# Layer one's first projections on raw transposed tokens, with rstd applied at their evictions

## The chip, the cores and the metric

The kernel runs on one core of a Trainium2 chip. The metric is the device time of one execution in microseconds (us), the median of several runs. Lower is better.

## What is computed

Two residual layers on 256 tokens of width 1024. Each layer normalizes the stream (RMS norm), makes one wide projection of it, and cuts this into three token mixers and their gates; the mixers' outputs are projected, gated, merged and projected again. What matters here is the beginning of a layer and the last norm:

```python
def rms_norm(x, w):
    y = x * lax.rsqrt(jnp.mean(x * x, axis=-1, keepdims=True) + NORM_EPS)
    return y * w

for layer in range(DEPTH):
    h = rms_norm(x, norm_w[layer])
    proj = jnp.einsum('bsd,de->bse', h, w_in[layer])
    (a_xbc, a_z, a_dt, b_q, b_k, b_v, b_z, c_q, c_k, c_v, c_f, c_z, gates) = jnp.split(proj, split_at, axis=-1)
    y_a = mamba2_branch(a_xbc, a_z, a_dt, ...)
    y_b = sliding_window_branch(b_q, b_k, b_v, b_z, ...)     # rope on q and k
    y_c = forgetting_attention_branch(c_q, c_k, c_v, c_f, c_z, ...)
    ...
    x = x + jnp.einsum('bsd,de->bse', merged, w_out[layer])
return rms_norm(x, final_norm_w)
```

The factor of a token, rstd = 1/sqrt(mean(x*x) + eps), is one number per token. A projection of h is therefore the projection of x * w, times rstd.

## The kernel before

**Products.** Every fp32 operand of a large product is cut into a high half (a rounded copy, `hi`, made by ScalarE) and a low half (the rest, `lo`, made by VectorE, in the start by POOL for a part), and a product is three passes: high by high, low by high, high by low. `split` (L254 to L263) does the cutting. The tokens stand transposed, channels on the partitions, in `hTh` and `hTl`, one block of 128 tokens after the other (t = 0, 1), eight blocks of 128 channels each (k). `tok` makes a product with tokens on the output's partitions (24 matmuls, 256 or 512 columns), `chan` one with channels there (24 matmuls of 256 columns).

**Weights.** The weights are a stream of parts of 128 x 1024 numbers (0.5 MB). SP's queue loads them (`load_to`, L328) into a ring of six tiles, `feed` (L358) splits them, at most AHEAD = 4 parts ahead of their use, and `release` (L376) gives a part back and feeds the next when its last product has read it. A piece of 256 columns is two parts, one of 512 columns four.

**Order.** TensorE's order is that of the program (`manual_schedule`). `ops` lists the products by hand. Small jobs (transposes of q and k, softmax groups, group norms) are generators put in by `launch` with a delay; `pump` enters those that are due at the end of a product, and in the middle of one with 512 columns, by a clock that the program keeps for TensorE. `drain` forces a branch's jobs to their end. For the start (up to and with the first value product) VectorE, ScalarE and POOL go by the program's order as well; behind it they are scheduled by the compiler.

**The start (L1134 to L1182).** SP's queue loads x's first 128 tokens, the norm weights as a row broadcast to all partitions, x's second 128 tokens, then weights. 30 transposes of the identity keep TensorE busy. The first tokens' squares give rstd (`row_rstd`, a power on POOL and four small VectorE steps), VectorE scales the tokens by it and by the norm row (L1160), TensorE transposes them, `split` writes `hTh` and `hTl`. The same follows for the second tokens, whose scaling POOL and ScalarE share (L1162 to L1176); their transposes stand inside the first key product (`second_rows`). `dense` with `after` groups that product's passes by four channel blocks and calls `second_rows` after each 12 matmuls. The first two weight parts are split in halves of two blocks, by ScalarE (L1148) and by VectorE and POOL (L1149).

**Layer one's order before:** sliding-window keys (256 columns, t = 0, 1), values, queries (two pieces of 512 columns, each t = 0, 1), the small projection for dt and the forget gate (`u_small`), the sliding window's gate z (four pieces, `u_z`), then eight conv pieces of 256 columns (`u_conv`), with the forgetting attention's values `u_cv` (two pieces of 512) behind the second and the fourth, the first gate behind the fifth, and `split_late` with the first branch projection behind the seventh. The evictions of keys and queries apply the rotary table (`rope`, L460 to L468, three VectorE products out of PSUM); those of values are ScalarE copies. A sliding-window group (`swa_quad`) may enter once the first z product is there.

**The end.** `out_end` (L988 to L1015) adds the residual, squares the new row pieces (ScalarE), and after the third piece computes rstd; in the last layer it multiplies 512 columns on VectorE and 512 on ScalarE and writes both.

Of the kernel before, what the change touches and what calls it, by code (L numbers as in the profile page):

```python
# [11 lines left out]
F32 = mybir.dt.float32  # L12
# [4 lines left out]
P = 128  # L17
# [14 lines left out]
WARM = 30  # L32
# [11 lines left out]
def hybrid_trunk(  # L44
# [110 lines left out]

    tab = T("tab", [P, 1])
# [3 lines left out]
    nwb0 = T("nwb", [P, D])  # L160
# [112 lines left out]
    def dense(pt, ah, al, bh, bl, w, after=None, mid=None):  # L273


        passes = ((ah, bh), (al, bh), (ah, bl))
# [50 lines left out]
    def load_to(j):  # L327

        while state["load"] < min(j, len(stream)):
# [3 lines left out]
            raw = T("raw" if n > 32 else "L1", [P, kper, n])  # L333
            for c, ap in src:
                m = ap.shape[-1]
                nc.sync.dma_start(raw[:, :, c:c + m],
                                  ap.rearrange("(k p) c -> p k c", p=P)[:, k:k + kper, :])
# [61 lines left out]
    y0.nwb = nwb0  # L399
# [42 lines left out]
    def tok(ah, al, w, t, turn=True, mid=None, **kw):  # L442
# [3 lines left out]
        p = pmm()  # L446
# [13 lines left out]
    def rope(p, t):  # L460

        p4 = p.rearrange("p (h d) -> p h d", h=4)
        cos = bc(rope_sb[:, t, 0, :], 1, 4)
        a = T("L1", [P, 4, 64])
        tt(a, p4, cos, op=ALU.mult)
        b = T("L1", [P, 4, 64])
        tt(b[:, :, 0:32], p4[:, :, 32:64], bc(rope_sb[:, t, 1, 0:32], 1, 4), op=ALU.mult)
        tt(b[:, :, 32:64], p4[:, :, 0:32], bc(rope_sb[:, t, 1, 32:64], 1, 4), op=ALU.mult)  # L468
        return a, b

    def u_bkv(y, c0, t, after=None):

        def f(w):
            p = tok(y.hTh, y.hTl, w, t, turn=w.n == 512 or c0 > 0, after=after)
# [4 lines left out]
            if c0 > 0:  # L479
                act(halves(y.bv[:, t, :]), p, AF.Copy)  # L480
            elif w.n == 512:
                act(y.bv[:, t, :], p[:, 1, :], AF.Copy)
            if c0 == 0:
                a, b = rope(p if w.n == 256 else p[:, 0, :], t)
# [3 lines left out]
                launch(1, rest(kd), D_K)  # L488
# [10 lines left out]
    def u_bq(y, c0, t):  # L499

        def f(w):
            p = tok(y.hTh, y.hTl, w, t, turn=w.n == 512)
            for i in range(w.n // 256):
                if t == 0:
                    y.qT[c0 + i] = T("qt", [P, 2, S])
                a, b = rope(p if w.n == 256 else p[:, i, :], t)
                q = T("L1", [P, 4, 64])
                gtt(q, a, b, op=ALU.add)
                launch(1, rest(c0 + i, q.rearrange("p h d -> p (h d)")), D_Q)
# [90 lines left out]
    def swa_quad(y, c, qT):  # L600
        yield lambda: (1, 0) in y.zdone
# [220 lines left out]
    def u_cv(y, c, t):  # L822
        def f(w):
# [3 lines left out]
            act(halves(y.cv[:, t, c:c + w.n]), p, AF.Copy)  # L827
# [160 lines left out]
    def out_end(y, c, t, i, n, xo, p):  # L988
        sl = slice(c, c + n)
        with tc.high_priority():  # L990
            tt(halves(y.xn[:, t, sl]), p, halves(xo), op=ALU.add)
            sum_sq(y.xn, t, c, y.ss[t][:, i:i + 1], n)
# [224 lines left out]
```

## Time and profile before

| | us |
|---|---|
| median of 3 runs (lowest to highest) | 848.27 (846.58 to 848.31) |
| the profiled execution | 847.65 |
| its span in the trace | 845.9 |
| granted TensorE clock in it | 0.996 |
| busy: PE, DVE, ACT, POOL | 833.4, 642.3, 511.6, 104.5 |

The span runs from the first recorded instruction to the end of the last transfer; the execution's own time is somewhat longer. Engines in the profile: PE is TensorE's matmuls, PEld its weight loads, DVE VectorE, ACT ScalarE, POOL GpSimd, SP the queue that loads weights. A busy PE is not a PE at its peak, since the ends of pipelined matmuls are modelled. A line of the timeline has start, length, engine, source line, operation, what it writes and reads (with a count), and in brackets the engine's idle time before it and what ended that.

### The profile page before, as it was taken

What the parts mean: (1) busy time and instruction counts of PE and PEld (TensorE: products, weight loads), DVE (VectorE), ACT (ScalarE), POOL (GpSimd) and SP (SyncE); (2) the same over time, 40 slices, a digit from 0 to 9 for tenths busy, and PEclk for the clock granted to TensorE, in tenths of its full rate; (3) what the DMA queues carried; (4) which work ended last, traced back from release to release, by engine and by line L of the source; (5) the groups of instructions that cost most, each with busy time, mean ns of one, the idle gap of its engine ahead of it and who ended that gap; (6) DMA issues with size and microseconds to landing.
All of it is one profiled execution on the core that took longest, in us unless ns stands there. A gap on an engine that the chain in (4) does not pass through costs nothing.

```text
span 845.9 us, 15985 instructions
## 1 busy us (share of the span) xinstructions
PE 833.4 (99%) x5964; PEld 763.3 (90%) x5964; DVE 642.3 (76%) x1403; ACT 511.6 (60%) x1004; POOL 104.5 (12%) x134
## 2 busy tenths in 40 slices
PE   7999999999999999999999999999999999999996
PEld 7999898989999998888989998899899999988896
DVE  5777997998776679656788879879968667785665
ACT  6466777665666667435555667776557667654442
POOL 6310100000131010210014001000003110121000
PEclk9999999999999999999999999999999999999999
DMA  8666565666465545648676465465755555576632
GB/s 303 183 205 208 166 200 162 201 210 197 128 202 175 172 159 187 218 155 282 206 237 218 143 206 159 142 199 183 241 171 176 174 175 152 161 235 212 212 100 76
DMA packets 126638, 158.43 MB, mean 187 GB/s; under 512 B 12784, under 2 KB 88224, under 8 KB 126560
## 3 DMA queue, kind: packets, MB, share of 16 engines
q1 hardware_dynamic: 109456, 140.79, 52.9%
q10 hardware_dynamic: 17056, 16.49, 6.4%
q8 instruction: 47, 0.77, 0.4%
q14 instruction: 31, 0.25, 0.1%
q0 software_dynamic: 48, 0.13, 0.0%
HBM read 155.22 MB, written 2.16 MB: 186 GB/s over the span
## 4 chain that ended last, share of the span: by engine, by line
PE 95%; DMA 2%; ACT 0%; DVE 0%; issue 0%; POOL 0%; SPq 0%; POOLq 0%; DVEq 0%; ACTq 0%
PE mm L96 82%; PE mx L96 9%; PE mx L100 4%; DMA raw<-in_w_proj_dram 2%; DMA raw<-in_w_in_dram 1%; POOL lo L1149 0%; ACT hi L1148 0%; ACT hi L259 0%; ACT L L1008 0%; DVE L L260 0%; DVE L L935 0%; DVE L L934 0%; ACT L L259 0%; POOLq L1213 0%; ACT L L215 0%
## 5 line engine op out<-in xcount | busy, mean ns | idle before, releaser
L260 DVE TENSOR_TENSOR lo<-raw,hi 128x1024 fp32r<-128x1024 f32 x252 | 308.2, 1234 | 94.9 <-ACT hi L259 81.9
L96 PE MATMUL mm<-hi,L 128*128 128x512 f32 (+1 forms) x1344 | 373.9, 364 | 1.9 <-ACT hi L1148 1.4
L259 ACT ACTIVATE hi<-raw 128x1024 fp32r<-128x1024 f32 x252 | 263.2, 1056 | 93.0 <-PE mm L96 66.9
L96 PE MATMUL mm<-L,hi 128*128 128x256 f32 x1792 | 317.7, 278 | 0.0
L96 PEld LDWEIGHTS mm<-L,hi 128*128 128x128 f32 x1792 | 277.7, 192 | 6.8 <-issue 3.3
L96 PEld LDWEIGHTS mm<-hi,L 128*128 128x128 f32 x1344 | 241.5, 190 | 32.4 <-issue 2.7
L96 PE MATMUL mm<-L,lo 128*128 128x256 f32 x896 | 246.4, 275 | 0.0
L96 PE MATMUL mm<-lo,L 128*128 128x512 f32 (+1 forms) x672 | 241.3, 360 | 0.6 <-POOL lo L1149 0.6
L96 PEld LDWEIGHTS mm<-L,lo 128*128 128x128 f32 x896 | 171.9, 192 | 0.2
L96 PEld LDWEIGHTS mm<-lo,L 128*128 128x128 f32 x672 | 127.3, 190 | 15.4 <-POOL lo L1149 0.8
L862 POOL TENSOR_SCALAR_AFFINE_SELECT bias<-bias 128x128 f32<-128x128 f32 x64 | 35.7, 593 | 407.8 <-DMA bias<-cumd 232.7
L556 ACT ACTIVATE pp<-pp,nm 128x128 f32<-128x128 f32 (+1 forms) x128 | 56.5, 443 | 13.0 <-DVE nm L550 13.0
L693 DVE SCALAR_TENSOR_TENSOR L<-L,vec,L 128x255 f32<-128x255 f32 (+2 forms) x96 | 46.3, 482 | 4.8 <-ACT L L690 3.4
L96 PE MATMUL mx<-L,L 128*64 128x128 f32 (+1 forms) x384 | 34.4, 314 | 0.0
L886 ACT ACTIVATE L<-L 128x512 f32<-128x512 f32 x24 | 15.2, 632 | 30.2 <-DVE L L885 30.0
L568 DVE TENSOR_SCALAR pp<-pp,rsum 128x128 f32<-128x128 f32 (+1 forms) x128 | 32.1, 314 | 0.5
L696 ACT ACTIVATE L<-L 128x256 f32<-128x256 f32 x32 | 13.3, 417 | 31.4 <-DVE L L693 25.9
L96 PEld LDWEIGHTS mx<-L,L 128*64 128x64 f32 x384 | 22.9, 136 | 9.4 <-ACT pp L556 1.3
L777 ACT ACTIVATE L<-mm 128x256 f32<-128x256 f32 x48 | 18.1, 378 | 21.0 <-PE mm L96 21.0
L585 ACT ACTIVATE L<-mx 128x512 f32<-128x512 f32 x48 | 27.0, 596 | 2.7 <-PE mx L100 2.5
L100 PE MATMUL mx<-ident,pp 128*128 128x128 f32 x192 | 26.3, 273 | 0.0
L100 PE MATMUL mx<-ident,L 128*128 128x128 f32 x152 | 23.1, 279 | 1.6 <-DVE L L935 0.8
(173 smaller groups left out, 716.0 us busy)
## 6 DMA issues: line engine op xcount, KB each, us to landing
raw<-in_w_in_dram SPq DMA_DIRECT2D x200, 512.0 KB, 4.3
raw<-in_w_proj_dram SPq DMA_DIRECT2D x48, 512.0 KB, 5.6
raw<-in_w_out_dram SPq DMA_DIRECT2D x16, 512.0 KB, 5.1
L<-cumd ACTq DMA_DIRECT2D x8, 512.0 KB, 5.2
bias<-cumd ACTq DMA_DIRECT2D x16, 256.0 KB, 3.8
L<-in_gate_bias_dram ACTq DMA_DIRECT2D x12, 256.0 KB, 3.9
L<-in_x_dram SPq DMA_DIRECT2D x2, 512.0 KB, 5.0
nwb<-in_norm_w_dram SPq DMA_DIRECT2D x1, 512.0 KB, 5.4
```

Of the source, the lines that this page charges most:

```text
L96: nc.tensor.matmul(o, a, b, **kw)
L100: nc.tensor.transpose(o, a, i)
L259: keep(act)(hi, src, AF.Copy)
L260: keep(tt)(lo, src, hi.bitcast(F32), op=ALU.subtract)
L556: act(pp[:, i, sl], pp[:, i, sl], AF.Exp, scale=-1.0, bias=nm[:, e:e + 1], accum_out=sums[:, e:e + 1])
L568: ts(pp[:, i, sl], pp[:, i, sl], rs[:, 2 * i + b:2 * i + b + 1], 0.5, op0=ALU.mult, op1=ALU.mult)
L585: act(pT, pt, AF.Copy)
L693: stt(a[:, s:S], x_[:, 0:S - s], y.vec[:, 16 * j + u:16 * j + u + 1], a[:, s:S], op0=ALU.mult, op1=ALU.add)
L696: act(th, a, AF.Tanh)
L777: act(halves(th), p, AF.Tanh, scale=0.5)
L862: nc.gpsimd.affine_select(out=bias[:, i, dst], in_=bias[:, i, src], compare_op=ALU.is_ge, fill=NEG, base=0, pattern=[[-1, P]], channel_mul ...
L886: act(g, g, AF.Tanh, scale=0.5)
```

## The change

**In the start.** The broadcast norm row is gone. The norm weights come as eight rows of 128 on ScalarE's queue, one small transpose puts them on the partitions (`nwT`). x's first tokens load in two halves, then the first two weight parts (the first in two halves), then x's second tokens, then weights. The raw x is transposed; VectorE multiplies the transposed block by `nwT` as it leaves PSUM (`turn`, into `xw`), ScalarE and VectorE cut `xw` into high and low half. The squares come behind, and rstd for all tokens (`y0.rn`) after the first key product. 10 warm-up transposes instead of 30, and 10 more between the two halves of the first tokens.

**At the evictions.** While `y.rn` is set, `rope` multiplies by rstd and the table in one three-operand step, and the value copies take rstd as their scale. This holds for keys, values, queries and the first piece of the forgetting attention's values, which moves up behind the queries.

**Later.** `normalize` (a job launched behind the queries) spreads rstd over the partitions with two fp32 products, multiplies `xw` by it in place and writes a second pair `hTh`, `hTl`; `normalized` drains it before the small projection and switches over.

**Layer one's order.** The conv pieces have the second value piece behind the third, the first gate behind the fifth, `split_late` behind the seventh and the second entry of the gate list behind the eighth. Sliding-window groups no longer wait for the first z product in layer one, but for the switch. Layer two keeps its order.

**In the end.** The last layer's last square is VectorE's, the variance goes ahead of the scaling by the norm row, and the two shares become 640 and 384 columns.

The diff, cut to its core:

```diff
-WARM = 30
+WARM = 10
+FILL = 10
...
+    nw8 = T("L1", [NK, P])
+    nc.scalar.dma_start(nw8, norm_w[0:1, :].rearrange("o (k p) -> (o k) p", p=P))
...
-    nc.sync.dma_start(x0[:, 0, :], x2[0:P, :])
-    nc.sync.dma_start(nwb0, norm_w[0:1, :].to_broadcast([P, D]))
-    nc.sync.dma_start(x0[:, 1, :], x2[P:S, :])
+    for j in range(2):
+        nc.sync.dma_start(x0[:, 0, j * 512:(j + 1) * 512], x2[0:P, j * 512:(j + 1) * 512])
...
             if after is not None:
-                if i % 12 == 11:
-                    after[i // 12]()
+                after.get(i + 1, lambda: None)()
...
+            if y.rn is None:
+                tt(o, i, bc(r, 1, 4), op=ALU.mult)
+            else:
+                stt(o, i, y.rn[:, t:t + 1], bc(r, 1, 4), op0=ALU.mult, op1=ALU.mult)
...
-                act(halves(y.bv[:, t, :]), p, AF.Copy)
+                act(halves(y.bv[:, t, :]), p, AF.Copy, scale=y.rn[:, t:t + 1])
...
-                launch(1, rest(kd), D_K)
+                launch(1, rest(kd), D_K if y.rn is None else 2 * D_K)
...
     def swa_quad(y, c, qT):
-        yield lambda: (1, 0) in y.zdone
+        yield lambda: (1, 0) in y.zdone or (y.l == 0 and y.rn is None)
...
-            sum_sq(y.xn, t, c, y.ss[t][:, i:i + 1], n)
             last = y.l + 1 == L
+            if last and i == 2:
+                junk = T("L2", [P, 512])
+                nc.vector.tensor_tensor_reduce(out=junk[:, 0:n], in0=y.xn[:, t, sl], in1=y.xn[:, t, sl],
+                                               scale=1.0, scalar=0.0, op0=ALU.mult, op1=ALU.add,
+                                               accum_out=y.ss[t][:, i:i + 1])
+            else:
+                sum_sq(y.xn, t, c, y.ss[t][:, i:i + 1], n)
...
-                    ts(y.xn[:, t, 0:512], y.xn[:, t, 0:512], r[:, 0:1], None, op0=ALU.mult)
+                    m = 640
+                    ts(y.xn[:, t, 0:m], y.xn[:, t, 0:m], r[:, 0:1], None, op0=ALU.mult)
...
-            op(k, u_bkv(y, 0, 0, [lambda j=j: second_rows(j) for j in range(2)]))
-            op(k, u_bkv(y, 0, 1))
+            op(k, u_bkv(y, 0, 0, {16: lambda: second_rows(0), 20: lambda: second_rows(1)}, lambda: first_end()))
+            op(k, u_bkv(y, 0, 1, {}))
...
+            op(None, lambda: launch(9, normalize(y0), 0.0))
+            op(cols(C_CV, 512), u_cv(y, 0, 0), u_cv(y, 0, 1))
+            op(None, lambda: normalized(y0))
...
+        if l == 0:
+            lights = {2: [lambda: cv(512)], 4: [gp.pop(0)], 6: [lambda: op(None, lambda y=y: split_late(y, 1))],
+                      7: [gp.pop(0)]}
+        else:
+            lights = {1: [lambda: cv(0)], 3: [lambda: cv(512)], 4: [gp.pop(0)], 6: [gp.pop(0)]}
...
+    def normalize(y):
+        rb = T("L1", [P, S])
+        for t in range(2):
+            act(rb[:, t * P:(t + 1) * P], ident, AF.Copy, scale=y.rn[:, t:t + 1])
+        yield 2.0
+        p = pmx()
+        for t in range(2):
+            mm(p[:, t * P:(t + 1) * P], ones, rb[:, t * P:(t + 1) * P], start=True, stop=True)
+        hTh = T("L8", [P, 2, NK, P], F32R)
+        hTl = T("L8", [P, 2, NK, P], F32R)
+        for t in range(2):
+            for k in (0, 4):
+                xk = xw[:, t, k:k + 4, :]
+                tt(xk, xk, bc(p[:, t * P:(t + 1) * P], 1, 4), op=ALU.mult)
+                split(hTh[:, t, k:k + 4, :], hTl[:, t, k:k + 4, :], xk)
+        y.normal = hTh, hTl
+        yield 0.0
+
+    def normalized(y):
+        drain(9)
+        (y.hTh, y.hTl), y.rn = y.normal, None
...
+        load_to(2)
+        nc.sync.dma_start(x0[:, 1, :], x2[P:S, :])
         load_to(N_RAW)
...
+        def turn(t, j):
+            p = pmx()
+            for k in range(4):
+                c = j * 512 + k * P
+                transpose(p[:, k * P:(k + 1) * P], x0[:, t, c:c + P], ident)
+            ks = slice(4 * j, 4 * j + 4)
+            tt(xw[:, t, ks, :], p.rearrange("p (k t) -> p k t", k=4), bc(nwT[:, ks], 2, P), op=ALU.mult)
...
+        square(0, 0)
+        turn(0, 0)
+        w_high(parts[0], 0)
+        high(0, 0)
+        turn(0, 1)
+        for i in range(FILL):
+            transpose(warm[:, 0:P], ident, ident)
+        low(0, 0)
+        w_high(parts[0], 2)
+        w_low(parts[0], 0)
+        w_low(parts[0], 2, gtt)
+        high(0, 1)
+        w_high(parts[1], 0)
+        low(0, 1)
+        w_low(parts[1], 0)
+        w_high(parts[1], 2)
+        w_low(parts[1], 2, gtt)
+        square(0, 1)
+
         def second_rows(j):
...
+            turn(1, j)
+
+        def first_end():
+            high(1, 0)
+            high(1, 1)
+            low(1, 0)
+            low(1, 1)
+            w_high(parts[2], 0)
+            w_high(parts[2], 2)
+            w_low(parts[2], 2, gtt)
+            w_low(parts[2], 0)
+            w_high(parts[3], 0)
+            w_high(parts[3], 2)
+            w_low(parts[3], 0)
+            square(1, 0)
+            square(1, 1)
+            w_low(parts[3], 2)
+            v = T("sm", [P, 8])
+            nc.vector.tensor_reduce(v[:, 0:2], ss.rearrange("p (t j) -> p t j", t=2), axis=mybir.AxisListType.X,
+                                    op=ALU.add)
+            ts(v[:, 0:2], v[:, 0:2], 1.0 / D, EPS, op0=ALU.mult, op1=ALU.add)
+            y0.rn = rsqrt(v, 2)
```

More of the change, by code (lines that the diff above doesn't have):

```diff
@@ L483, in f @@
             if c0 == 0:
-                a, b = rope(p if w.n == 256 else p[:, 0, :], t)
+                a, b = rope(y, p if w.n == 256 else p[:, 0, :], t)
                 kd = T("L2", [P, 4, 2, 64])
@@ L826, in f @@
                 y.cv = T("L8", [P, 2, D])
-            act(halves(y.cv[:, t, c:c + w.n]), p, AF.Copy)
+            act(halves(y.cv[:, t, c:c + w.n]), p, AF.Copy, scale=1.0 if y.rn is None else y.rn[:, t:t + 1])
             pump()
@@ new lines, in high, with low, w_high, w_low @@
+        def high(t, j):
+            ks = slice(4 * j, 4 * j + 4)
+            act(y0.hTh[:, t, ks, :], xw[:, t, ks, :], AF.Copy)
+        def low(t, j):
+            ks = slice(4 * j, 4 * j + 4)
+            tt(y0.hTl[:, t, ks, :], xw[:, t, ks, :], y0.hTh[:, t, ks, :].bitcast(F32), op=ALU.subtract)
+        def w_high(part, k):
+            raw, hi, _ = part
+            act(hi[:, k:k + 2, :], raw[:, k:k + 2, :], AF.Copy)
+        def w_low(part, k, sub_=tt):
+            raw, hi, lo = part
+            sub_(lo[:, k:k + 2, :], raw[:, k:k + 2, :], hi[:, k:k + 2, :].bitcast(F32), op=ALU.subtract)
@@ new lines, in square @@
+        def square(t, j):
+            sum_sq(x0, t, 512 * j, ss[:, 2 * t + j:2 * t + j + 1], 512)
+        parts = [new_part() for _ in range(4)]
+        square(0, 0)
[12 more added lines that the diff above has]
+        low(0, 1)
```

101 lines of the change are left out of this document (38 added, 63 removed).

## The prediction

> **What bounds the kernel now.** I read the page's span and the engines' shares of its chain first, then the view of PE's waits (us in total, times, longest), then the last matmul.
>
> ```profile
> span 845.9 us, 15985 instructions
> PE 95%; DMA 2%; ACT 0%; DVE 0%; issue 0%; POOL 0%; SPq 0%; POOLq 0%; DVEq 0%; ACTq 0%
> ```
>
> ```profile
> PE mx L100 <- POOL ident masks.py:199: 1.5, 1, 1.5
> PE mm L96 <- ACT hi L1148: 1.4, 1, 1.4
> PE mx L100 <- DVE L L935: 0.8, 1, 0.8
> PE mx L100 <- DVE L L1160: 0.7, 1, 0.7
> PE mm L96 <- POOL lo L1149: 0.6, 1, 0.6
> ```
>
> ```profile
> 838.74 0.28 PE L96 MATMUL mm<-lo,L 128*128 128x256 f32 x1
> ```
>
> The reader is to see that TensorE carries 95% of the chain and that its waits are few: those on the identity, L1160, L1148 and L1149 lie in the start, one of 0.8 (L935) where layer one ends; at the other end the last matmul is over at 839.02 and the span at 845.9. An edit in the middle can win next to nothing and can lose; a gain has to come from the start and the tail. The start in stretches of 2 us:
>
> ```profile
> 2.00:4.00 2.00, 2.00 (x11) 2.00 (x11) 0.00 (x0) 0.28 (x2) 1.99 (x8) 1.00 0.65 258
> 6.00:8.00 2.00, 1.30 (x12) 1.06 (x10) 1.48 (x6) 0.00 (x0) 0.35 (x1) 1.00 1.02 391
> 10.00:12.00 2.00, 1.33 (x9) 1.12 (x10) 1.90 (x7) 2.00 (x4) 1.17 (x2) 1.00 1.10 347
> 12.00:14.00 2.00, 1.37 (x8) 1.17 (x7) 1.17 (x2) 1.26 (x3) 2.00 (x2) 0.75 1.09 355
> 14.00:16.00 2.00, 2.00 (x12) 2.00 (x11) 0.08 (x1) 1.32 (x3) 1.90 (x2) 0.50 1.06 390
> ```
>
> Columns are the stretch, its length, busy time (count) of PE, PEld, DVE, ACT, POOL, then granted clock, DMA share, GB/s. From 6 us on the DMA engines are full; TensorE's work is thin until 14 and then runs at half clock (0.50). What it waits for, and a mark to measure by:
>
> ```profile
> 4.47 0.63 ACT L215 ACTIVATE L<-L 128x512 f32<-128x512 f32 x1 [2.18 <-DMA L<-in_x_dram]
> 8.03 0.63 ACT L215 ACTIVATE L<-L 128x512 f32<-128x512 f32 x1 [2.83 <-DMA L<-in_x_dram]
> 2.18 7.77 DMA raw<-in_w_in_dram
> 9.98 1.15 ACT L1148 ACTIVATE hi<-raw 128x512 fp32r<-128x512 f32 x2
> 10.66 1.50 PE L96 MATMUL mm<-hi,L 128*128 128x256 f32 x8 [1.38 <-ACT hi L1148]
> 11.20 1.76 POOL L1149 TENSOR_TENSOR lo<-raw,hi 128x512 fp32r<-128x512 f32 x1 [0.83 <-ACT hi L1148]
> 25.56 0.60 PE L100 MATMUL mx<-ident,L 128*128 128x128 f32 x4
> 17.36 8.36 PE mm L96 x72
> ```
>
> The first product (10.66) waits for the weight part's high half (9.98), and that for the part's DMA, landed at 2.18 + 7.77 = 9.95. It is fourth in SP's queue, behind x, the broadcast norm row and x. My mark is 25.56, when the four products of keys and values are through and the 512-wide query products come next. 72 matmuls in 8.36 us are 0.116 each: a product of 24 takes 2.8 us, so four need 11.1 us and the start loses some 14.
>
> **The change, part by part. The head's DMA.** The queue lands 0.5 MB at 4.47, 1.5 MB at 8.03 and 2.0 MB at 9.95, about 1.8 us for each half MB. Without the 0.5 MB norm row, and with weights ahead of the second tokens, straight lines between these points give: first weight half (0.75 MB) 5.4, second 6.3, next part 8.0, second tokens 9.95, third and fourth part 11.9 and 13.8 (an estimate from those three rows). The norm row comes instead as 4 KB on ACT's queue ahead of everything; I cost it at nothing, because the first scaling cannot start before x's first half (about 3.6) has been transposed; if it lands after 4.4, everything waits as long (0 to 1 us).
>
> **The head's work**, by these durations:
>
> ```profile
> 9.40 0.15 DVE L219 TENSOR_REDUCE sm<-ss 128x1 f32<-128x2 f32 x1 [0.83 <-ACT L L215]
> 11.05 0.16 DVE L209 TENSOR_TENSOR rs<-sm,sm 128x1 f32<-128x1 f32 x1
> 11.13 0.69 DVE L1149 TENSOR_TENSOR lo<-raw,hi 128x512 fp32r<-128x512 f32 x1
> 19.24 0.42 DVE L465 TENSOR_TENSOR L<-mm,rope 128x256 f32<-128x256 f32 x1
> 19.77 0.28 DVE L468 TENSOR_TENSOR L<-mm,rope 128x128 f32<-128x128 f32 x1
> ```
>
> Without rstd ahead of it, ACT makes the first high halves at 5.4 to 6.6 (0.6 each), so the first product can start near 6.7 instead of 10.66. It does not run through: POOL's low half (1.76 us, after a high half at 7.2) holds passes until 9.0, the second tokens (9.95) hold the transposes placed inside the product, and it ends near 12.1. The second key product then waits for VectorE: four scalings and four low halves of tokens and two low halves of weights, 10 x 0.69 = 6.9 us, three of the scalings and low halves only after the transposes; done at 13.8. It ends at 15.4, the two value products at 18.2 and 21.0.
>
> The new wait is rstd at the evictions. ACT's last two squares stand behind everything else: the second transposes (11.6), their scaling and high half (12.9) and four high halves of weights (0.57 each, 15.2); at 0.63 each, the length of the square at 4.47, they end at 16.5. From reduce to rstd took 9.40 to 11.21, 1.8 us, so rstd comes at 18.4. Two rotary evictions follow (19.24 to 20.05, 0.8 each; I price the three-operand form like the two-operand one) and free the banks by 20.1 to 20.4. Queued behind them on VectorE is the query weight's first low half (1.2 us, 21.6), which TensorE wants at 21.4. On ACT the first value eviction waits for rstd too (18.4 against the product's end at 18.2); the query weights' high halves are emitted ahead of it, so nothing that TensorE needs soon stands behind. POOL's sums of the rotated keys come later by as much, and their transposes are put off by the doubled delay, behind the first query product. So the mark moves to about 21.2: **4.4 us won**. Bounds: four products and eight transposes straight behind a start at 6.7 would end at 18.6 (7 won); with half the clock over the first products, only 1.5 (half of 3.2 us at half clock, and rstd 1.3 late with it).
>
> **The clock.** Warm-up goes from 30 transposes to 20 in two groups. In the rows above 11 transposes fill 2 us (2:4), later 12 take 1.30 us (6:8): they got faster under transposes alone, and after the thin stretch the clock fell to 0.50. I take no loss, since the new stretch of 6.7 to 9.0 is as thin as 10:12 was, but shorter. The Trainium skill (TensorE: Matmul & The Clock Gate, Part 1) says that one idle window of about 3.4 us brings the half rate back; here the clock fell (14:16) after a stretch in which TensorE was two thirds busy (10:14), so the trace is the stricter of the two. The same page (Part 4) says that transposes don't count as activity for this; 2:4 against 6:8 speaks against it. By that rule the whole first product would be cold, the rival below.
>
> **Normalizing later.**
>
> ```profile
> 316.82 0.61 PE L96 MATMUL mx<-L,ones 128*128 128x128 f32 x4
> 317.19 0.68 PE L96 MATMUL mm<-hi,L 128*128 128x512 f32 x2
> L260 DVE TENSOR_TENSOR L<-mx,L 128x512 fp32r<-128x512 f32 x8 | 5.4, 687 | 3.6 <-ACT L L259 3.4
> 29.19 10.36 PE mm L96 x48
> 40.00:50.00 10.00, 10.00 (x59) 8.94 (x59) 5.26 (x12) 3.86 (x7) 3.32 (x4) 1.00 0.64 201
> ```
>
> TensorE gets two fp32 products, which occupy 0.4 us (316.82 to 317.19): +0.4 on the path. VectorE gets eight of 0.69 us, 5.5 us. They are emitted after the moved value product's first half, so the second half (24 x 0.216 = 5.2 us) covers them; VectorE had 4.7 us free in 40 to 50. The small projection behind needs all of it and its own split: 0.5 + 5.5 + 0.4 against 5.6 leaves **0.8 us** of wait (0, if VectorE takes them at once, to 3).
>
> **The moved order.** The value piece leaves the place between conv pieces, so three of these come in a row.
>
> ```profile
> L260 DVE TENSOR_TENSOR lo<-raw,hi 128x1024 fp32r<-128x1024 f32 x252 | 308.2, 1234 | 94.9 <-ACT hi L259 81.9
> L693 DVE SCALAR_TENSOR_TENSOR L<-L,vec,L 128x255 f32<-128x255 f32 (+2 forms) x96 | 46.3, 482 | 4.8 <-ACT L L690 3.4
> L697 DVE SCALAR_TENSOR_TENSOR L<-L,L 128x256 f32<-128x256 f32 x32 | 13.4, 420 | 3.6 <-ACT L L696 3.6
> 54.71 0.34 DVE L550 CUSTOM_DVE_ANT_0 pp<-mx,wmask,nsink 128x128 f32<-128x128 f32 x1
> 60.28 0.41 DVE L780 SCALAR_TENSOR_TENSOR L<-L,mm 128x256 f32<-128x256 f32 x1
> 50.00:130.00 80.00, 80.00 (x644) 72.88 (x642) 70.57 (x217) 58.54 (x155) 5.59 (x10) 1.00 0.60 186
> ```
>
> A conv piece costs VectorE 2 x 1.23 + 2 x (3 x 0.48 + 0.42) = 6.2 us against 5.6 on TensorE; three are 1.8 short, and with a head group's softmax (54.71 to 60.28, 5.6 us) in them over 4. Weights are split four parts ahead: a piece's first part is asked for when the piece two before it is half through its second channel unit, 1.4 + 5.6 = 7 us before use, of which high and low half take 2.3. So a lag of 4.7 us is free. I take 0.5 us (0 to 3). The late split one piece earlier, and the sliding-window groups that start one product earlier, I cost at nothing: no wait of TensorE stands there now, and the last conv piece covers the split. The three more large tiles (scaled tokens, second pair of transposed tokens) make eight of eight buffers with the values; x and the first pair are free again before the z pieces ask, so I cost that at nothing; if not, the first z piece waits.
>
> **The tail.**
>
> ```profile
> 839.51 0.42 ACT L215 ACTIVATE L<-L 128x256 f32<-128x256 f32 x1 [1.69 <-DVE L L991]
> 840.39 0.15 DVE L1003 SCALAR_TENSOR_TENSOR sm<-ss,sm 128x1 f32<-128x1 f32 x1
> 841.73 0.72 ACT L1008 ACTIVATE L<-L,rs 128x512 f32<-128x512 f32 x1 [1.71 <-DVE rs L230]
> ```
>
> The last square is now ACT's (839.51), with its readout and VectorE's scaling ahead of the variance at 840.39. On VectorE, straight behind the add (which ends when the square starts), it lets the variance start near 840.0 if it takes the same 0.42: 0.4. The 640/384 cut takes some 0.1 off ACT's 0.72, and the larger transfer may give it back. **0.4 won** (0.2 to 0.5).
>
> **Sum:** -4.4 - 0.4 + 0.4 + 0.8 + 0.5 = -3.1 us, on the profiled execution's 847.65 us (span 845.9 and 1.75 around it): 844.5. That execution lies 0.6 under the median 848.27; on the median the sum gives 845.2, which I predict.
>
> **The rivals.** (1) *No waits inside*: VectorE's spare time takes the normalizing and the three conv pieces, and the head does a little better; -4.4 to -6, 842 to 844. For it: TensorE waits nowhere in the middle now. Chance 0.20. (2) *Half clock over the first products*, 3.2 us of it as at 13 to 16: it costs half of that, 1.6 us, and rstd and the query weights slip with it; -1.4, 846.9. Against it: less idle time than now. Chance 0.13. (3) *The start stays bound*: rstd or a transfer comes 3 us later than worked out, so the banks are freed late and most of the head's gain is gone; it would do less than it says, about 0, 848. Chance 0.07. (4) *Slower*: VectorE doesn't work off the normalizing in the z pieces. Then 5.5 us meet the three conv pieces 4.6 us short, and past the free lag of 4.7 TensorE waits 5.4, with 1.5 at the small projection; -4.8 + 0.4 + 6.9 = +2.5, 850.8. It decides once VectorE's lag passes 4.7 us. For it: VectorE is busy 70.57 of the 80 us from 50 to 130, and the same work has 11 us less of TensorE's time to lie under. Chance 0.15.
>
> **How the numbers follow.** The forecast, with terms inside their bounds (843.5 to 846.5), has 0.45. Range 842 to 849.3: it leaves out the worst of (4) and the best of (1). Faster by over 0.2% (1.7 us; about what can be told from no change) is the forecast, (1) and a part of (2): 0.70. Within: the rest of (2) and (3), 0.15. Slower: 0.15.
>
> **What would show it.** First 256-wide product near 6.7 and the 512-wide query products near 21; the two evictions behind rstd at about 18.4; a PE wait at the small projection under 1 us; none on low halves in the three conv pieces; granted clock 1.00 after 8 us. The prediction is wrong if PE's waits on low halves in 50 to 130 sum to over 3 us, or if the query products start after 23.

## The result, and the profile after

The changed kernel takes 851.83 us (median of 9 runs, 850.39 to 855.18), the kernel before 848.0 beside it (846.58 to 848.68): a ratio of 1.0051 [1.0035, 1.0066], slower by half a per cent. The prediction was 845.2, within 842.0 to 849.3.

The profiled execution took 850.39 us. Its page begins so, and its chain of waits has these shares:

```profile
span 848.7 us, 15975 instructions
PE 94%; DMA 2%; DVE 2%; ACT 1%; issue 1%; POOL 0%; SPq 0%; POOLq 0%; DVEq 0%; ACTq 0%
```

The span is 2.8 us longer, and TensorE has lost a per cent of the chain to VectorE and ScalarE. The head, first its one row in the view of stretches, then three lines of the timeline:

```profile
0.00:20.00 20.00, 17.36 (x118) 15.75 (x119) 11.54 (x22) 13.61 (x26) 8.23 (x21) 1.00 0.90 302
```

```profile
7.02 0.50 PE L97 MATMUL mx<-hi,L 128*128 128x256 f32 x2
19.37 0.16 DVE L210 TENSOR_TENSOR rs<-sm,sm 128x2 f32<-128x2 f32 x1
21.72 0.60 PE L97 MATMUL mm<-hi,L 128*128 128x512 f32 x2
```

The head does what it was worked out to do: first product at 7.02 (10.66 before), and the mark, the first 512-wide query product, at 21.72. Its place before was 25.91, straight behind the transposes at 25.56. The clock column has 1.00, but it has that too where only slow transposes stand: nine from 1.79 on take 2.13 us, ten from 5.81 on 1.42, so the full rate comes at about 6 us, just ahead of the first product. Some 4.2 us are won up to the mark, and the loss lies behind it. PE's waits name the place:

```profile
PE mx L101 <- POOL L L515: 4.2, 1, 4.2
PE mx L101 <- POOL ident masks.py:199: 1.5, 1, 1.5
PE mm L97 <- DVE lo L261: 1.0, 1, 1.0
PE mx L97 <- ACT hi L1217: 0.8, 1, 0.8
```

One wait of 4.2 us, at transposes of q, for POOL's sum. The timeline around it (ACT, then DVE, then PE):

```profile
43.57 1.06 ACT L260 ACTIVATE hi<-raw 128x1024 fp32r<-128x1024 f32 x1 [8.89 <-PE mx L101]
44.66 1.22 DVE L261 TENSOR_TENSOR lo<-raw,hi 128x1024 fp32r<-128x1024 f32 x1 [6.92 <-ACT hi L260]
45.80 0.99 DVE L473 SCALAR_TENSOR_TENSOR L<-mm,rs,rope 128x256 f32<-128x256 f32 x3
47.72 0.69 PE L101 MATMUL mx<-ident,L 128*128 128x128 f32 x2 [4.20 <-POOL L L515]
```

Read from the end: the transposes wait for POOL's sum, this for a rotary eviction (45.80) of a query product that has long been done, and the eviction stands on VectorE behind a low half (44.66) that waited 6.92 us. ScalarE, whose high half that is, stood 8.89 us. The bracket names PE, whose transposes ended at 43.52, just ahead of it. But the part of the weight stream that this high half reads was asked for at 30.76 and landed only at 43.47. In the kernel without the transfers found below (a2_dskip_cut) the same part, asked for at 30.24, has landed at 34.02, and the high half starts at 34.29, long before those transposes. So it is the transfer that this wait is for. The stretches show it:

```profile
30.00:32.00 2.00, 2.00 (x11) 1.71 (x10) 1.77 (x3) 1.82 (x4) 0.73 (x1) 1.00 0.67 223
32.00:34.00 2.00, 2.00 (x13) 1.81 (x12) 2.00 (x5) 1.81 (x3) 1.04 (x1) 1.00 0.05 0
38.00:40.00 2.00, 2.00 (x12) 1.76 (x11) 0.00 (x0) 0.00 (x0) 0.55 (x1) 1.00 0.03 0
42.00:44.00 2.00, 1.52 (x9) 1.07 (x7) 0.00 (x0) 0.43 (x1) 0.00 (x0) 1.00 1.05 405
48.00:50.00 2.00, 2.00 (x7) 1.62 (x7) 1.89 (x6) 2.00 (x5) 0.40 (x1) 0.50 1.05 348
```

The last two columns are the DMA engines' busy share and GB/s. From 32 to 40 us next to nothing is moved, and the engines are hardly busy either (0.03 to 0.05). Behind the wait the clock is 0.50: another 1.4 us or so. What ScalarE's queue sent off just ahead of the hole, in the timeline, and the same tile in the page's list of DMA issues (count, KB each, median us to landing):

```profile
27.52 1.59 ACTq L255 DMA_DIRECT2D dsk<-in_d_skip_dram  x2
```

```profile
dsk<-in_d_skip_dram ACTq DMA_DIRECT2D x4, 2.0 KB, 8.9
```

These are the `d_skip` constants, two transfers in each layer. `layer_consts` takes every second value of a row and broadcasts it to 64 partitions, so each transfer of 2 KB is 512 separate pieces of four bytes. The change does not touch them. The kernel before has the same hole, in its timeline and its stretches:

```profile
32.22 1.34 ACTq L254 DMA_DIRECT2D dsk<-in_d_skip_dram  x2
```

```profile
34.00:36.00 2.00, 2.00 (x11) 1.76 (x10) 0.82 (x1) 2.00 (x4) 0.17 (x1) 1.00 0.08 9
36.00:38.00 2.00, 2.00 (x11) 1.76 (x10) 2.00 (x3) 1.99 (x3) 0.00 (x0) 1.00 0.04 0
```

There the parts that it delays belong to the gate z. Its first piece, needed at 50.3 us, has its two parts ahead of the hole's effect; the delayed ones are those of the second (from its second part on) and of the third. The high half of a part of the third piece, and that piece's first matmul:

```profile
49.40 1.06 ACT L259 ACTIVATE hi<-raw 128x1024 fp32r<-128x1024 f32 x1 [2.75 <-DMA raw<-in_w_in_dram]
64.44 0.36 PE L96 MATMUL mm<-L,hi 128*128 128x256 f32 x1
```

ScalarE waits for the part, but the products begin only at 64.44, and those of the second piece, whose late high half started at 45.58, at 58.43: over ten us of slack are left. After the change the queries would be through at about 45 and the moved value piece is next; its second part is there only at 43.47, some 13 us after it was asked for, and the eviction that PE needs stands behind it. **Theory T**: the four-byte pieces stop the weight stream; the change made the cover too short. It does so in two ways at once: the head is 4.2 us faster, and behind the queries comes a 512-wide piece, which needs its four parts within some 5 us, instead of z, which takes two in 5.4. No run here tells their shares apart. **Rivals**: R, the stream stops for another reason; V, VectorE's order, with a rotary eviction behind a low half, is the fault whatever the transfers do; O, the moved order itself costs the time.

### The profile page after: what moved, and what is told of

Its sections match the earlier page's. It is cut to its first block, busy times and chain, and to the rows that moved or that the text cites. A ratio compares the mean times of both kernels' runs of the same rounds, so it can differ in the third digit from the quotient of the medians.

```text
span 848.7 us, 15975 instructions
## 1 busy us (share of the span) xinstructions
PE 833.3 (98%) x5959; PEld 761.6 (90%) x5959; DVE 651.7 (77%) x1411; ACT 510.8 (60%) x1006; POOL 101.0 (12%) x130
## 4 chain that ended last, share of the span: by engine, by line
PE 94%; DMA 2%; DVE 2%; ACT 1%; issue 1%; POOL 0%; SPq 0%; POOLq 0%; DVEq 0%; ACTq 0%
PE mm L97 80%; PE mx L97 9%; PE mx L101 4%; DMA raw<-in_w_proj_dram 1%; DVE lo L261 1%; DMA raw<-in_w_in_dram 1%; DVE L L473 0%; ACT hi L1217 0%; ACT hi L260 0%; DVE lo L1221 0%; POOL lo L1221 0%; SPq L164 0%; POOL sm L204 0%; POOL L L515 0%; DVE L L1205 0%
## 5 line engine op out<-in xcount | busy, mean ns | idle before, releaser
L97 PEld LDWEIGHTS mm<-hi,L 128*128 128x128 f32 x1328 | 238.8, 190 | 30.9 <-issue 2.2
L97 PEld LDWEIGHTS mm<-lo,L 128*128 128x128 f32 x664 | 125.5, 190 | 16.9 <-DVE lo L261 2.4
L101 PE MATMUL mx<-ident,L 128*128 128x128 f32 (+1 forms) x153 | 24.0, 284 | 4.3 <-POOL L L515 4.2
```

The source lines that it names most:

```text
L97: nc.tensor.matmul(o, a, b, **kw)
L101: nc.tensor.transpose(o, a, i)
```

## The experiments

Ratios are to the kernel before, with 95% intervals.

### Move the pieces, or remove them

Moved: layer one's two transfers go behind the gate columns, in a function of their own.

```diff
         zs(C_ZB, 1)
+        if l == 0:
+            op(None, lambda: skip_consts(y0))
```

> The changed kernel with layer one's two d_skip transfers (512 pieces of four bytes each) issued after the small projection and the gate columns instead of with the other constants. Theory T (these transfers hold up the weight stream from 32 to 40 us, so the second part of the value piece lands late, the rotary eviction queued behind it on VectorE is late, and PE waits 4.2 us at the transposes of q and then runs some 3 us at half clock): no stretch of near-zero DMA between 32 and 40, the 4.2 us wait at those transposes gone, the clock 1.00 through 45-50, and 851.8 - 4.2 - 1.4 = 846.2 us (845 to 847.5), ratio to the kernel before about 0.998. Rival R (the transfer rate falls there for another reason: the small piece's 64-byte rows or the number of transfers in flight): the outage and the wait stay, 851 to 852, ratio 1.004 to 1.005. Rival V (VectorE's order alone: the rotary eviction stands behind low halves whatever the transfers do): the stream flows but PE still waits 1 us or more there, 848 to 850.

852.18 us, 1.0058 [1.0039, 1.0076]: no gain. The first hole is gone, and so is the wait at the transposes, but a hole and a wait of PE are found again at the new place (timeline, then stretches; in a2_dskip_cut the stretch from 90 to 100 moves 253 GB/s):

```profile
89.71 0.66 ACTq L255 DMA_DIRECT2D dsk<-in_d_skip_dram  x1
...
106.72 0.58 PE L97 MATMUL mm<-L,hi 128*128 128x256 f32 x1 [5.25 <-ACT L L702]
```

```profile
90.00:100.00 10.00, 10.00 (x93) 10.00 (x92) 6.02 (x16) 3.96 (x7) 0.00 (x0) 1.00 0.04 0
...
105.00:110.00 5.00, 3.27 (x15) 3.28 (x16) 4.93 (x10) 4.11 (x10) 3.07 (x6) 0.59 0.80 244
```

The wait of 5.25 us goes back to VectorE, which waits 8.8 us for a small transfer (`cumd`) that ScalarE's queue sends off at 91.19, behind the pieces: not the weight stream alone is held up. The number that T gave was wrong, since it took the new place for covered; the hole that goes along with the transfers is what T needs. R would have left the hole where it was.

Removed, in both layers: `d_skip` comes as a fifth 16-wide row beside four others, and two small VectorE copies cut it.

```diff
-        y.hb = T("hb", [P, 64], bufs=2)
-        for i, v in enumerate((dt_bias, f_bias, sinks, a_log)):
+        y.hb = T("hb", [P, 80], bufs=2)
+        for i, v in enumerate((dt_bias, f_bias, sinks, a_log, d_skip)):
...
-            pdma(y.dsk[64 * half:64 * half + 64, :], src.to_broadcast([64, NK]))
+            pin(ts)(y.dsk[hp, :], y.hb[hp, 64:80].rearrange("p (j two) -> p two j", two=2)[:, half, :], 1.0, None,
+                    op0=ALU.mult)
```

> The changed kernel with no four-byte transfers at all: d_skip comes as a fifth 16-wide row beside the four others and two small VectorE copies cut it, in both layers. Theory T: as with the transfers moved, 846.2 us (844.5 to 847.5), the wait of 4.2 us at the transposes of q gone and no outage between 32 and 40 us; some tenths more may come where layer two's two transfers stood. Rival R: outage and wait stay, 851 to 852. Rival V: stream flows, PE waits 1 us or more there, 848 to 850. If this one is clearly better than the moved transfers, these cost something at their new place too.

843.48 us, 0.9949 [0.9938, 0.9961]: 8.4 us under the changed kernel, more than expected: the wait of 4.2 and the half clock behind it make 5.6, and the rest is not assigned (the profiled executions differ by 6.8, and the changed kernel's median is 1.4 above its own). Stretches and PE's longest waits behind the identity's:

```profile
32.00:34.00 2.00, 2.00 (x11) 1.76 (x10) 1.76 (x2) 1.81 (x3) 2.00 (x1) 1.00 0.97 343
38.00:40.00 2.00, 2.00 (x11) 1.76 (x10) 0.81 (x3) 0.96 (x3) 1.05 (x2) 1.00 1.05 347
```

```profile
PE mx L97 <- DVE lo L1222: 0.9, 1, 0.9
PE mm L97 <- DVE lo L261: 0.9, 1, 0.9
```

The stream runs through, and no wait is left behind the head. V alone falls: the compiler's order still has the low half ahead of the eviction, and nothing waits.

The same edit on the kernel before:

> The kernel before with the same edit of d_skip (no four-byte transfers, both layers). There the outage of 35 to 45 us is in the trace too, but the parts that it delays are those of the gate columns, needed at 50 us, and PE waits for none of them. Theory T: outage gone, time within 0.5 us of the kernel before, ratio 0.9995 to 1.0005; if layer one's or two's transfers cost it something hidden, up to 1 us faster. If it gains as much as the changed kernel does from the same edit (5 us), the transfers' cost does not hang on what was moved, and the change itself is at fault in some other way.

846.20 us, 0.9980 [0.9971, 0.9988]: 1.8 us faster, more than T gave and far less than the 8.4. Its profile no longer has the wait of 0.8 us at the end of layer one (L935); of the other 1.0, some 0.6 stands in the start (the mark is at 25.28 instead of 25.91, and the clock from 14 to 16 us is 1.00 instead of 0.50), which lies ahead of the pieces' issue at 32.22, so that it is not shown to be theirs. The same edit is worth 1.8 before the change and 8.4 after. And this gives a clean pair: **843.48 against 846.20, the change without them is worth -2.7 us.**

### VectorE's order alone

```diff
-                stt(o, i, y.rn[:, t:t + 1], bc(r, 1, 4), op0=ALU.mult, op1=ALU.mult)
+                pin(stt)(o, i, y.rn[:, t:t + 1], bc(r, 1, 4), op0=ALU.mult, op1=ALU.mult)
...
-            split(hi, lo, raw, keep=pin if state["pin"] else lambda f: f)
+            split(hi, lo, raw, keep=pin if state["pin"] or y0.rn is not None else lambda f: f)
```

> The changed kernel with its transfers as they are; the rotary evictions and the splits of the query stage are kept in the order in which the program names them, so that no low half of the value piece stands ahead of the second rotary eviction of the second query product. Theory T with VectorE's order as the link: the outage of 32 to 40 us stays, but the wait at the transposes of q falls from 4.2 to below 0.5, and PE waits for the value piece's second part only at its own product, about 1 us or less: 851.8 - 4.2 - 1.4 + 1 = 847.2 us (846 to 849). If the outage alone decides whatever the order, PE's wait only moves to the value product's low halves and the time stays 850 to 852. The first query product should also lose part of its 1.7 us of stretching if its low halves come in another order; here their order is the same, so 6.9 us from 21.7 stays.

846.22 us, 0.9987 [0.9972, 1.0002]: 5.6 us back with the transfers untouched. In its stretches:

```profile
35.00:40.00 5.00, 5.00 (x27) 4.37 (x26) 3.71 (x8) 2.99 (x5) 1.48 (x2) 1.00 0.29 24
40.00:45.00 5.00, 5.00 (x27) 4.39 (x26) 4.18 (x8) 0.98 (x3) 3.22 (x2) 1.00 0.69 255
45.00:50.00 5.00, 5.00 (x27) 4.39 (x26) 3.37 (x6) 3.04 (x6) 0.23 (x1) 1.00 1.10 353
```

The hole is there (24 GB/s), and PE is busy all the time at full clock. The other 2.7 us against a2_dskip_cut are only in part explained: the profiled execution took 849.22 and has a PE wait of 2.36 us from 385 to 388, in layer two, for a VectorE step, with half clock behind it. In layer one both are needed for the 4.2 us: a late part, and an eviction queued behind it. Taking away either one removes the wait.

### How many pieces, of what size, on whose queue

Half of layer one's pieces (one transfer of 512, none in layer two), and all 1024 of layer one with none in layer two; in both, the rest of `d_skip` is cut as above.

> The changed kernel with d_skip cut from the constants in layer two and in half of layer one: one transfer of 512 four-byte pieces is left at its place in layer one (two had 1024). Theory T by pieces (each piece costs the stream a share of the outage): the stretch without transfers after it is about half as long, some 4 to 5 us instead of 8 to 9, the value piece's second part lands about 4 us sooner, and PE's wait at the transposes of q falls from 4.2 to 0 to 0.5 us without half clock: 843.5 to 844.5 us. Rival by transfers (a transfer of this kind has a latency of 8.7 us whatever its count, and the stream stands for that long): the outage stays near 8 us, PE waits about 4 us, 848 to 849.5.

> The changed kernel with d_skip cut from the constants in layer two alone; layer one's two transfers of 1024 pieces stay. With neither the time was 843.5, with both 851.8. Theory T puts 5.6 us on layer one (4.2 wait, 1.4 half clock at the transposes of q), so 843.5 + 5.6 = 849.1 us (848 to 850.4) here, and the rest, about 2.7 us on the average and uneven from run to run (a wait at about 387 us, 0.2 to 2.4 us in the profiles, with half clock behind it), on layer two: the spread of 850.4 to 855.2 should shrink to under 1.5 us. If layer two's transfers cost nothing, 851 to 852 with the same spread.

845.82 us, 0.9969 [0.9957, 0.9980], and 851.65 us, 1.0038 [1.0025, 1.0050]. The stretches of c1_half, then of c2_layer_two_cut:

```profile
32.00:34.00 2.00, 2.00 (x11) 1.76 (x10) 2.00 (x4) 1.81 (x3) 1.49 (x1) 1.00 0.05 1
34.00:36.00 2.00, 2.00 (x11) 1.73 (x11) 2.00 (x2) 0.22 (x1) 0.15 (x1) 1.00 0.03 0
36.00:38.00 2.00, 2.00 (x13) 1.76 (x12) 1.28 (x4) 0.00 (x0) 0.64 (x1) 1.00 0.47 163
```

```profile
32.00:34.00 2.00, 2.00 (x12) 1.76 (x11) 2.00 (x5) 2.00 (x4) 1.14 (x1) 1.00 0.05 1
...
40.00:42.00 2.00, 2.00 (x11) 1.75 (x10) 0.00 (x0) 0.00 (x0) 0.00 (x0) 1.00 0.09 22
```

The one hole lasts 4 us, the other 8 to 10, with a wait of 5.5 us at the same transposes. The rival by transfers falls. Half the pieces cost 1.3 us more than I expected: two waits at those transposes are left, 0.94 and 1.35. And layer two's pieces are worth nothing that the medians of the changed kernel show, where I had put 2.7 on them: layer one's alone make up 8.2. What did come is the smaller spread, 851.35 to 852.27 in five runs against 850.39 to 855.18 in nine, so layer two's pieces may cost some executions something; no run shows it alone.

Twice as many, in the kernel before (layer two's cut, a second pair to a tile that nothing reads):

```diff
+        if l == 0:
+            again = T("again", [P, NK])
+            for half in range(2):
+                src = d_skip[l:l + 1, :].rearrange("o (j two) -> two o j", two=2)[half]
+                pdma(again[64 * half:64 * half + 64, :], src.to_broadcast([64, NK]))
```

> The kernel before with layer two's d_skip cut and layer one's two transfers issued twice over (2048 pieces; the second pair goes to a tile that nothing reads). With none at all it took 846.2 us and lost nothing to one pair in layer one beyond what hides. Theory T by pieces: the stretch without weight transfers from about 33 us doubles to 16 to 18 us, the gate columns' first parts, which just made it at 50 us, land some 8 us later, PE stands for 5 to 8 us about there and goes to half clock behind it: 851 to 856 us. Rival (the kernel before is proof against it since nothing stands behind a late part there): 846 to 847.

858.86 us, 1.0124 [1.0110, 1.0137], 12.7 over the same kernel without any, and past my upper end.

```profile
34.00:40.00 6.00, 5.33 (x27) 4.45 (x25) 0.00 (x0) 0.33 (x1) 0.00 (x0) 1.00 0.06 4
44.00:54.00 10.00, 8.82 (x39) 7.07 (x38) 7.24 (x16) 3.49 (x7) 3.82 (x4) 0.90 0.05 0
60.00:65.00 5.00, 1.92 (x8) 1.20 (x8) 3.77 (x9) 3.47 (x9) 1.57 (x1) 0.81 1.10 348
```

The hole is 16 us now, in two, and PE stands at 60 to 65:

```profile
63.03 1.92 PE L96 MATMUL mx<-L,qt 64*128 64x128 f32 x8 [3.36 <-ACT qt L529]
```

That is again an eviction (`qt`, ScalarE's) queued behind a high half that waited 7.98 us for its part. The kernel before was not proof against the hole; it had cover for one pair of transfers and not for two. Hole by pieces in layer one: none at 0, 4 us at 512, 8 to 10 at 1024, 16 at 2048; 8 to 10 ns for each piece.

On GpSimd's queue instead of ScalarE's (`nc.gpsimd.dma_start`, layer one's 1024, layer two's cut):

> The changed kernel with layer two's d_skip cut and layer one's two transfers of 1024 four-byte pieces issued on GpSimd's queue instead of ScalarE's, at the same place of the program. On ScalarE's queue this took 851.7 us, without them 843.5. If the pieces themselves stop the weight stream, whoever issues them: a stretch of near zero of 8 us again somewhere behind about 25 us, PE's wait of about 5 us at the transposes of q, 850 to 852. If it is ScalarE's and SyncE's issuing that stands in each other's way: no such stretch, 843.3 to 845. A third way: GpSimd itself is held by issuing them, and its sums for q behind it come late; then the stream flows, and PE waits for GpSimd's sums, 845 to 850.

850.25 us, 1.0021 [1.0009, 1.0033].

```profile
30.00:38.00 8.00, 8.00 (x42) 6.88 (x41) 4.27 (x6) 3.92 (x5) 2.34 (x2) 1.00 0.60 0
```

```profile
PE mx L101 <- POOL L L523: 4.2, 2, 2.4
```

The hole is the same 8 us with 0 GB/s, and most of the loss. So it isn't ScalarE's issuing; and GpSimd is not held itself, since its sums there wait for VectorE's evictions. One thing differs: here the engines count as 0.60 busy in the hole, with ScalarE's queue as 0.04.

The same number of pieces on ScalarE's queue, 64 bytes each (columns of a weight matrix into a tile that nothing reads; `d_skip` cut):

> The changed kernel with d_skip cut in both layers (843.5 us) and, where layer one's two transfers stood, two others of the same number of pieces on the same queue, 2 times 512, but 64 bytes each (columns of a weight matrix into a tile that nothing reads). If the number of pieces decides: the stretch of 8 us without weight transfers is back, PE stands 4 to 5.5 us, 850 to 852. If their smallness or how they are spread over the engines decides: the stream dips by 2 us or less, as behind the small projection's own 2048 rows of 64 bytes, and the time is 843.3 to 845.

843.93 us, 0.9948 [0.9933, 0.9962], like no such transfers.

```profile
30.00:38.00 8.00, 8.00 (x43) 7.00 (x42) 7.13 (x11) 5.93 (x7) 2.38 (x2) 1.00 0.93 273
```

Not the number of pieces makes the hole, but that number of four-byte ones (these also read different places, where `d_skip`'s read the same 64 bytes over and over; which of the two counts is open). The Trainium skill (DMA: Bandwidth & Descriptors, Rules for kernel authors) says that a transfer whose last dimension is strided becomes one descriptor for each element, and to make that dimension contiguous. The trace agrees: 2 KB in 512 pieces land after 8.9 us, the contiguous rows that replace them, 8 KB in 128 copies, after 5.4. The Trainium skill (same page, Anatomy of one DMA) calls the cost of making descriptors on GpSimd's path small, with room for many before it shows; f1_gpsimd_queue has an 8 us hole with 1024 of them, though no run tells whether making or moving them takes the time.

### The tail alone, and the order alone

The tail's edits on the clean kernel before:

> The kernel before with d_skip cut in both layers (846.2 us) and of the change only its tail: the last sum of squares on VectorE, the order of the small operations, the last scaling cut at 640 instead of 512. My forecast for the tail was -0.4 (0.2 to 0.5): 845.8 us (845.6 to 846.0), a ratio of 0.9975 to the kernel before. The clean pair differ by 2.7 us in all, so the head and the order would then be worth 2.3. If the tail gives nothing, 846.2.

845.97 us, 0.9971 [0.9960, 0.9981], 0.2 under its base, which the intervals do not tell from 0. The last issue of the span, of b1_dskip_cut_before and of g1_tail_clean_before:

```profile
837.04 0.28 PE L96 MATMUL mm<-lo,L 128*128 128x256 f32 x1
840.78 0.34 ACTq L1010 DMA_DIRECT2D out_dram<-L  x1
```

```profile
837.10 0.28 PE L96 MATMUL mm<-lo,L 128*128 128x256 f32 x1
840.38 0.36 ACTq L1018 DMA_DIRECT2D out_dram<-L  x1
```

From the last matmul to the last issue 3.74 us become 3.28: 0.46. Up to the end of the span only some 0.2 to 0.3 of it is left.

The moved order undone on the clean changed kernel, for theory O:

```diff
-            op(cols(C_CV, 512), u_cv(y, 0, 0), u_cv(y, 0, 1))
             op(None, lambda: normalized(y0))
...
+            lights = {1: [lambda: cv(0)], 3: [lambda: cv(512)], 4: [gp.pop(0)],
+                      6: [lambda: op(None, lambda y=y: split_late(y, 1)), gp.pop(0)]}
```

> The changed kernel with d_skip cut in both layers (843.5 us), and with the kept tokens normalized straight behind the queries, ahead of the small projection, the first value piece back between the convolution pieces and the attention bias split as before. This undoes the moved order alone. Then nothing lies over the normalizing: of its 5.5 us on VectorE and ScalarE 3 to 5 stand before the small projection, with some half clock behind them: 843.5 + 3 to 6.5 = 846.5 to 850 us, taken at 848.3. If the moved order had itself been the loss (the rival that three conv pieces in a row overload VectorE), this would be 843 or faster.

853.68 us, 1.0062 [1.0050, 1.0075]: 10.2 over the clean changed kernel, well past my range.

```profile
45.00:50.00 5.00, 1.66 (x9) 1.02 (x7) 4.87 (x10) 2.43 (x7) 1.83 (x2) 1.00 0.92 281
50.00:55.00 5.00, 2.23 (x9) 1.75 (x9) 4.30 (x8) 2.46 (x4) 0.47 (x1) 0.56 0.43 139
55.00:60.00 5.00, 4.98 (x36) 4.05 (x36) 2.59 (x17) 1.90 (x8) 0.00 (x0) 0.76 0.00 0
```

PE is busy 3.9 of the 10 us from 45 to 55 and then at 0.56 and 0.76 of the clock. Theory O falls with it, on the kernel without the pieces: there the moved order does not cost the time, it saves some 10 us. The row from 55 to 60 also has next to no transfers, without any four-byte piece: no weight part is issued there between 49.1 and 64 us, so none was asked for.

### What is left in the head, and the best version

In the clean changed kernel the first query product takes 7.1 us instead of some 5.2, since VectorE's low halves stand behind rstd and two rotary evictions. Here these evictions and the sums behind them (now kept in `later`) go behind the first two low halves, and the keys' transposes are put off by three times the delay instead of twice:

```diff
         release(pieces[0], 2)
+        for f in later:
+            f()
         run_op(*ops[2])
```

> The changed kernel without four-byte transfers (843.5 us), and with the two rotary evictions of the key product put behind the low halves of the first query piece's first two parts on VectorE. The first query product now takes 6.9 us instead of 5.2 for waits on low halves; the first of these would end at 20.2 instead of 22.05 and the product should take 5.2 to 5.6. The key's sums on GpSimd end about 2.4 us later, at 27.2, and their transposes come at about 26.6: up to 0.6 us given back there. 843.5 - 1.6 + 0.3 = 842.2 us (841.6 to 843.0). Rival (the product's pace is set by the low halves' own rate, four of 1.2 us, and the wait only moves to its later parts or to the second product): 843.2 to 843.8.

842.29 us, 0.9926 [0.9912, 0.9940], 1.2 under its base and the fastest of all. In its timeline one wait is left in that product, of 0.42 where 0.94 was:

```profile
25.45 0.48 PE L97 MATMUL mm<-lo,L 128*128 128x512 f32 x1 [0.42 <-DVE lo L261]
```

## Why the prediction was wrong, point by point

- **The head, -4.4: right at the mark, short behind it.** In the clean pair the mark goes from 25.28 to 21.12, 4.2 us. But "queued behind them on VectorE is the query weight's first low half" was priced as one step that comes at 21.6. rstd was there at 19.5 and not at 18.4, each of the two evictions took 1.0 and not 0.8, the first low half was a microsecond late, and the three behind it follow at 1.2 us each: the product lost 1.7, in the clean kernel 1.9. d1_lows_first brought 1.2 of it back. Net, the head is worth about -2.3.
- **The clock: right.** The full rate was there from about 6 us on and the first product ran with it, so the rival of a cold first product fell. Only transposes had run until then, which speaks once more against the Trainium skill's rule that they don't count (TensorE: Matmul & The Clock Gate, Part 4). The Trainium skill's idle window of about 3.4 us (same page, Part 1) fits only in part: after 4.20 us idle the clock was 0.50, and after 0.94 and 1.35 in c1_half it stayed at 1.00, but in a3_rotary_first it fell to 0.50 about a microsecond after a wait of 2.36 us. As in the start of the kernel before, the trace is the stricter of the two.
- **Normalizing, +0.4 and +0.8: the products right, the wait 0.** With or without the hole (with it, behind the wait of 4.2 us) PE was busy up to the small projection. The moved value piece covers it all.
- **The moved order, +0.5: in itself nothing.** No wait in the three conv pieces; the slower rival, VectorE's backlog of 5.4 us, didn't come.
- **The tail, -0.4: right as far as the trace shows it**, 0.46 up to the last issue; the medians differ by 0.2, which is not told from 0.
- **The failed step: "Weights are split four parts ahead: a piece's first part is asked for [...] 7 us before use [...]. So a lag of 4.7 us is free."** It took for granted that a part lands a few microseconds after it is asked for. In the changed kernel's view of its weight transfers issued from 30 to 45 us stands:

```profile
DMA to landing us min/median/max: 12.7/13.5/14.3
```

In a2_dskip_cut the median of the same is 6.5. Without the pieces the median is 843.48, with them 851.83. The sum had no term for this. The hole was in the profile of before (9 and 0 GB/s at 34 to 38 us), and I read PE's waits there, found none, and wrote "no wait of TensorE stands there now". The wait was absent since the parts that the hole delays were needed only from 58.4 us on. Without the pieces the sum of -3.1 comes near a measured -2.7, in part by luck: the head brought some 2 us less than its term, and the 1.3 us priced for waits didn't come. With them the kernel before takes 1.8 longer and the changed one 8.4: -2.7 + 8.4 - 1.8 = +3.9, which only says again, from the same medians, what was measured (3.8). My signs of failure (waits on low halves between 50 and 130, query products after 23) never came: they looked at the wrong place. And the time lies near the slower rival's 850.8, but not by its mechanism.

## What to carry to other kernels

Look for holes in the transfers' row, not only for waits. First see whether work was asked for and not landed, since a row near zero can also mean that nothing was asked for; such a hole that nobody waits for is slack used up, and a faster stage ahead of it or an earlier need behind it may turn it into a wait. Work out for each part of a stream when it lands against when it is used, and take that slack, not the absence of a wait, as the cover. Where a small strided load of many four-byte pieces stands beside a stream that matters, try the contiguous row, cut on chip: here that was worth 8.4 us. And don't queue an eviction that somebody waits for behind a split whose input may be late.

## What the runs showed of the hardware

Two transfers of 2 KB each, in four-byte pieces, stop a stream that otherwise runs at some 350 GB/s, for 8 us, whether ScalarE or GpSimd issues them; 1024 pieces of 64 bytes do nothing of the kind. By what mechanism is open. With ScalarE's queue the engines' mean share in the hole is 0.03 to 0.05, which would be 0.5 to 0.8 of one engine in sixteen, as if one engine had all the pieces and every other transfer waited for its share there; with GpSimd's queue the share is 0.60, which does not fit that picture. The traces' records of packets differ too: from ScalarE's queue they are of four bytes and about 7 ns each, some 100 starting per us; from GpSimd's each transfer is 16 packets of 128 bytes that last 3.6 to 3.8 us. They don't name the engine, and no run tells the mechanisms apart.
